# Moving 228 stores from SyncE's DMA queue to GpSimd's, and spreading eight squares over 14 steps

## The chip, the cores and the metric

The kernel runs on one core of one Trainium2 chip. The metric is the device time of one execution in microseconds (us). Three runs of the kernel before took 1536.45, 1539.39 and 1541.62 us, a median of 1539.39. The engines are named as the profile names them: PE (TensorE, matmuls; PEld are its weight loads), DVE (VectorE), ACT (ScalarE), POOL (GpSimd) and SP (SyncE, which here does nothing but issue DMAs).

## The reference

A decoder block on `x` (1 x 2048 x 1024, float32), one layer:

```python
xn = rms_norm(h, norm_w)                     # over 1024 features
proj = xn @ w_in                             # 1024 x 5632
u_a, z_a, q_b, f_b, i_b, og_b, z_b, g_a, g_b = split(proj)
y_a = s5_branch(u_a, z_a, ...)   # diagonal complex scan, GELU, GLU, times silu(z_a)
y_b = hgrn2_branch(q_b, f_b, i_b, og_b, z_b, ...)  # 4 gated recurrent heads, head norm, silu(z_b)
merged = sigmoid(g_a) * (y_a @ w_proj_a) + sigmoid(g_b) * (y_b @ w_proj_b)
h = h + merged @ w_out
return rms_norm(h, final_norm_w)
```

## The kernel before, in words

The 2048 tokens are worked in two halves `a` = 0 and 1 of 1024, each in two blocks `b` of 512. Matmuls run in float32r: every operand is split into a high and a low part (`split`, L118: ACT makes the high part at L119, DVE the low part at L120), and a product is three matmuls (high-high, high-low, low-high).

Projection. The columns of `w_in` are 22 slices of 256. The first two or three slices of the first half are done plainly (`plain`); all others by one level of Strassen's scheme (`strassen`, L425): seven products per slice, each one step of the dense loop with 12 matmuls (L458 to L460). Each product takes one weight operand of 128x1024, made by `w_ops` (L370) three products ahead, in a ring of five buffers (tag `wo`). In the first half `w_ops` makes the operands from raw weights (loads at L383) and also stores each to DRAM (`wc_d`, L391); the second half only loads them back (L375). PSUM banks are emptied on ACT by `snap` (L464), which copies a bank into an SBUF tile (`u`, `s`).

Tokens. The token statistics of a half are sums of squares: `norm_stats` (L178) loads rows of `xn` (L190) and squares them on ACT with a running sum (L191); `newton_rsqrt` (L149) on DVE makes the scale; `norm_diag` and `norm_bcast` spread it with one matmul. `xprep` (L239) then loads two tiles of transposed tokens (L243, L244; tag `y`, a ring of two buffers of 128x1024), scales them and forms the seven Strassen operands. For the first half they are split at once; for the second half they are stored to DRAM (`xo_d`, L257) and loaded back later by `x_load` (L287).

Other intermediate results also go through DRAM: the z gates (`silu_evac`, L863), the S5 output after GELU (`gelu`, L851), the state carried from the first half to the second (`hgrn_block`, L1042), the head outputs (`hgrn_fin`, L1084) and the b-branch part of the merge (`merge_b`, L1150). The sigmoid gates (`sg_d`, L875) and the S5 inputs and outputs are stored from ACT's queue. All other DMAs are issued from SP's queue.

Order. PE's instructions run in the order in which the program is written (`manual_schedule`, L1412); for the other engines and for the DMA queues a planner orders the instructions by priority and expected time, and each engine and queue then works strictly in order. The dense loop is a generator, and `timed` (L1372) runs background pieces (heads, statistics, token preparation) at numbered steps of it. For the first half's loop, the statistics of the second half's tokens come at steps 2 and 8 (L1482), their broadcasts at 13 and 18, and `xprep` of the second half from step 20 on. The kernel reserves 1024 bytes of SBUF per partition for descriptors of GpSimd's DMA queue, and issues no DMA there.

Of the kernel before, what the change touches and what calls it, by code (L numbers as in the profile page):

```python
# [11 lines left out]
F32 = mybir.dt.float32  # L12
# [3 lines left out]
AF = mybir.ActivationFunctionType  # L16
ALU = mybir.AluOpType
# [4 lines left out]
D = 1024  # L22
HALF = 1024
# [8 lines left out]
def hybrid_block(  # L32
# [24 lines left out]
    nc = tc.nc  # L57
    V = nc.vector
    S = nc.scalar
# [40 lines left out]
    def y4(name):  # L100
        return yp.tile([128, 1024], F32, name=name, tag="y")
# [13 lines left out]
    def r2(name, dt=F32R):  # L115
        return rp.tile([128, 512], dt, name=name, tag="r")
# [61 lines left out]
    def norm_stats(a, b):  # L178
        t0 = a * HALF + b * 512
        c0 = a * 8 + b * 4  # L180
        for i in range(4):
            rows = slice(t0 + i * 128, t0 + (i + 1) * 128)
            if a == 0:
                for h in range(2):
                    xr = r2(f"xr{a}{b}{i}{h}", F32)
                    nc.sync.dma_start(xr, xn[rows, h * 512 : h * 512 + 512])
                    S.activation(xr, xr, AF.Square, accum_out=ssh[:, h * 4 + i : h * 4 + i + 1])
            else:
                xr = y4(f"xr{a}{b}{i}")
                nc.sync.dma_start(xr, xn[rows, :])  # L190
                S.activation(xr, xr, AF.Square, accum_out=ssx[:, c0 + i : c0 + i + 1])  # L191
        if a == 0:
            V.tensor_tensor(ssx[:, c0 : c0 + 4], ssh[:, 0:4], ssh[:, 4:8], op=ALU.add)
        newton_rsqrt(ssx[:, c0 : c0 + 4], 4, 1.0 / D, rst[:, c0 : c0 + 4])

    def norm_diag(a, b):
        c0 = a * 8 + b * 4
# [41 lines left out]
    def xprep(a, k, rbs):  # L239
        t0 = a * HALF  # L240
        xa = y4(f"xa{a}{k}")
        xb = y4(f"xb{a}{k}")
        nc.sync.dma_start(xa, xt[k, :, t0 : t0 + HALF])  # L243
        nc.sync.dma_start(xb, xt[k + 4, :, t0 : t0 + HALF])  # L244
        (b11, b12), (b21, b22) = ((t[:, 0:512], t[:, 512:1024]) for t in (xa, xb))

        def scale(v, kk, b):
            V.scalar_tensor_tensor(v, v, nw_t[:, kk : kk + 1], rbs[b], op0=ALU.mult, op1=ALU.mult)

        def op(p, raw):  # L250
            n = f"X{a}{k}{p}"
            if a == 0:
                hi, lo = r2(n + "h"), r2(n + "l")
                split(raw, hi, lo)
                X[a][p][k] = (hi, lo)
            else:
                nc.sync.dma_start(xo_d[p][k // 2][:, (k % 2) * 512 : (k % 2) * 512 + 512], raw)  # L257

        scale(b11, k, 0)
        op(0, b11)  # L260
        yield
        scale(b21, k + 4, 0)
        op(1, b21)
        yield
        scale(b12, k, 1)
        scale(b22, k + 4, 1)
        yield
        t3 = sn(f"t3x{a}{k}")
        V.tensor_tensor(t3, b22, b12, op=ALU.subtract)
        V.tensor_tensor(b12, b12, b11, op=ALU.subtract)  # L270
        yield
        V.tensor_tensor(b11, b12, b22, op=ALU.subtract)
        op(2, b11)
        yield
        op(3, b12)
        yield
        op(4, t3)
        yield
        V.tensor_tensor(b21, b21, b11, op=ALU.add)
        op(5, b21)  # L280
        yield
        op(6, b22)
        yield
# [86 lines left out]
    def w_ops(a, sl):  # L370
        n = f"{a}_{sl}"
        if sl in wc_d:
            for p in range(7):
                t = wo4(f"w{n}_{p}")
                nc.sync.dma_start(t.bitcast(F32), wc_d[sl][p])  # L375
                yield t
            return
        if a == 0:
            wc_d[sl] = [dram.tile([128, 1024], F32, name=f"wc{sl}_{p}") for p in range(7)]

        def get(kh):
            raw = (y4 if a and sl != SL_VO else wr4)(f"rw{n}_{kh}").rearrange("p (k n) -> p k n", k=4)
            nc.sync.dma_start(raw, wi[sl, kh])  # L383
            return raw[:, :, 0:128], raw[:, :, 128:256]

        def op(p, raw):
            t = wo4(f"w{n}_{p}")
            v = t.rearrange("p (i k n) -> p i k n", i=2, k=4)
            split(raw, v[:, 0], v[:, 1])
            if a == 0:  # L390
                nc.sync.dma_start(wc_d[sl][p], t.bitcast(F32))  # L391
            return t

        a11, a21 = get(0)
        yield op(0, a11)
        a12, a22 = get(1)
        s1 = wpool.tile([128, 4, 128], F32, name=f"s1{n}", tag="wt", bufs=2)
        s2_ = wpool.tile([128, 4, 128], F32, name=f"s2{n}", tag="wt", bufs=2)
        t = op(1, a12)
        V.tensor_tensor(s1, a21, a22, op=ALU.add)  # L400
        yield t
        V.tensor_tensor(s2_, a11, s1, op=ALU.subtract)
        yield op(2, s2_)
        t = op(3, s1)
        V.tensor_tensor(a11, a11, a21, op=ALU.subtract)
        yield t
        t = op(4, a11)
        V.tensor_tensor(a12, a12, s2_, op=ALU.add)
        yield t
        yield op(5, a22)  # L410
        yield op(6, a12)
# [425 lines left out]
    def gelu(a, i):  # L837
        ya = wr4(f"ya{a}{i}")
        yy = y4(f"yy{a}{i}").rearrange("p (t c) -> p t c", t=8)
        nc.sync.dma_start(yy, y_d[a][i].rearrange("t p g c -> (p g) t c"))  # L840
        for i4 in range(4):
            c0 = i4 * 256
            dst = ya[:, c0 : c0 + 256] if i4 % 2 == 0 else ya[:, c0 + 255 : (c0 - 1 if c0 else None) : -1]
            S.activation(dst.rearrange("p (c t) -> p t c", t=8), yy[:, :, i4 * 32 : i4 * 32 + 32], AF.Copy)
        q = yy.rearrange("p t c -> p (t c)")
        S.activation(q, ya, AF.Square)
        V.tensor_scalar(q, q, 0.044715, 1.0, op0=ALU.mult, op1=ALU.add)
        V.tensor_tensor(q, q, ya, op=ALU.mult)
        S.activation(q, q, AF.Sigmoid, scale=GE)
        V.tensor_tensor(ya, ya, q, op=ALU.mult)  # L850
        nc.sync.dma_start(ft_d["ya", a, i], ya)  # L851

    def silu_evac(nm, a, i):
        def evac(ft, b, ps, sb):
            f = i * 2 + ft
            s = ps if sb is None else sb
            e = sn(f"e{nm}{a}{f}{b}")
            S.activation(e, s, AF.Sigmoid)
            if nm == "zb":
                V.scalar_tensor_tensor(e, s, hnw_t[:, f : f + 1], e, op0=ALU.mult, op1=ALU.mult)  # L860
            else:
                V.tensor_tensor(e, e, s, op=ALU.mult)
            nc.sync.dma_start(ft_d[nm, a, f][:, b * 512 : b * 512 + 512], e)  # L863

        return evac

# [66 lines left out]
    def hgrn_block(a, h, b):  # L933
# [105 lines left out]
            pv = ch(st, c)  # L1039
        st_prev[0] = pv  # L1040
        if a == 0 and b == NBLK - 1:
            nc.sync.dma_start(carry_d[h], pv)  # L1042
        yield
        ps = psm.tile([128, 512], F32, name=f"po{n}", tag="psm")
        for c in range(4):
# [20 lines left out]
    def hgrn_fin(a, h, direct=None):  # L1066
        o8 = (h % 2) * 8
        y = []
        for b in range(NBLK):
            y.append(sn(f"zy{a}{h}{b}"))  # L1070
            nc.sync.dma_start(y[b], ft_d["zb", a, h][:, b * 512 : b * 512 + 512])
        yield
        for b in range(NBLK):
            ys = h2(f"ys{a}{h}{b}", "x")
            for c in range(4):
                i = o8 + b * 4 + c
                S.activation(ch(ys, c), ch(OO[a, h, b], c), AF.Copy, scale=rso[:, i : i + 1])
            yield
            ps = psm.tile([128, 512], F32, name=f"py{a}{h}{b}", tag="psm")
            for c in range(4):  # L1080
                nc.tensor.transpose(ch(ps, c), ch(ys, c), ident)
            V.tensor_tensor(y[b], y[b], ps, op=ALU.mult)
            if direct is None:
                nc.sync.dma_start(ft_d["yb", a, h][:, b * 512 : b * 512 + 512], y[b])  # L1084
            else:
                direct(b, y[b])
            yield
# [26 lines left out]
    def merge_b(a):  # L1114
# [21 lines left out]
        for i, (jj, f, b) in enumerate(tiles):  # L1136
# [10 lines left out]
            mac12(ps, w, slice(f * 128, f * 128 + 128), [YB[a, k, b] for k in range(4)], (3,) if jj == 0 else range(4))  # L1147
            sg = sgs.pop(i)
            V.tensor_tensor(sg, sg, ps, op=ALU.mult)
            nc.sync.dma_start(ft_d["mb", a, j][:, b * 512 : b * 512 + 512], sg)  # L1150
            if i % 4 == 3:
                w = wn
            yield
# [244 lines left out]
    def steps(ev, g, at):  # L1398
        for t in at:
            ev.append((t, lambda: step(g)))  # L1400
        ev.append((at[-1], lambda: run(g)))
# [10 lines left out]
    with tc.manual_schedule(engines={mybir.EngineType.PE}):  # L1412
# [59 lines left out]
        def bcast(b):  # L1472
            rb1[b] = norm_bcast(1, b, dg1[b])
# [1 line left out]
        dg1 = {}  # L1475

        def stats(b):
            norm_stats(1, b)
            dg1[b] = norm_diag(1, b)

        ev = heads(0, 3, 35, 18)
        ev += [(2, lambda: stats(0)), (8, lambda: stats(1)), (13, lambda: bcast(0)), (18, lambda: bcast(1))]  # L1482
        xg = chain(*[xprep(1, k, rb1) for k in range(4)])
        steps(ev, xg, [20 + (s * 92) // 35 for s in range(36)])
        for i in range(6):
# [158 lines left out]
```

## Time and profile before

| | |
|---|---|
| median of three runs | 1539.39 us (1536.45 to 1541.62) |
| the profiled execution's own time | 1540.05 us |
| its span, first to last instruction | 1538.3 us |
| PE, PEld busy | 1467.0, 1207.3 us |
| DVE, ACT, POOL busy | 1100.8, 637.6, 3.6 us |
| mean granted TensorE clock | 0.984 |
| moved by DMA | 354.53 MB, 230 GB/s over the span |
| DMAs of SP and ACT (shares of 16 DMA engines) | 63.6%, 4.8% |

The profile is of one execution. Busy time is the union of an engine's instructions. A view of waits says for how long an engine stood idle before an instruction, and whose end released it. The granted clock is a share of TensorE's full speed: 1.00 is 2.4 GHz, 0.50 is 1.2 GHz, and a stretch between them held both. The DMA share is the mean busy share of the 16 DMA engines.

### The profile page before, as it was taken

What the parts mean: (1) busy time and instruction counts of PE and PEld (TensorE: products, weight loads), DVE (VectorE), ACT (ScalarE), POOL (GpSimd) and SP (SyncE); (2) the same over time, 40 slices, a digit from 0 to 9 for tenths busy, and PEclk for the clock granted to TensorE, in tenths of its full rate; (3) what the DMA queues carried; (4) which work ended last, traced back from release to release, by engine and by line L of the source; (5) the groups of instructions that cost most, each with busy time, mean ns of one, the idle gap of its engine ahead of it and who ended that gap; (6) DMA issues with size and microseconds to landing.
All of it is one profiled execution on the core that took longest, in us unless ns stands there. A gap on an engine that the chain in (4) does not pass through costs nothing.

```text
span 1538.3 us, 21386 instructions
## 1 busy us (share of the span) xinstructions
PE 1467.0 (95%) x7360; PEld 1207.3 (78%) x7360; DVE 1100.8 (72%) x2409; ACT 637.6 (41%) x1391; POOL 3.6 (0%) x24
## 2 busy tenths in 40 slices
PE   7997999999999999999989999999989899899997
PEld 5776788788888777878878887788878688688886
DVE  5798688678678659956665887776649877765445
ACT  7456454454454634323323455333353332532222
POOL 0000000000000000000000000000000000000000
PEclk9998999999999999999999999999999999999999
DMA  9539778977977883786668559677977854854602
GB/s 336 175 115 305 284 278 295 316 255 269 331 264 286 285 271 119 186 245 197 231 201 313 174 163 294 217 259 264 327 236 234 266 184 137 274 171 131 212 14 103
DMA packets 192060, 354.53 MB, mean 230 GB/s; under 512 B 65680, under 2 KB 74896, under 8 KB 191952
## 3 DMA queue, kind: packets, MB, share of 16 engines
q1 hardware_dynamic: 163792, 328.00, 63.6%
q10 hardware_dynamic: 28160, 25.17, 4.8%
q8 instruction: 58, 0.95, 0.3%
q14 instruction: 50, 0.41, 0.1%
HBM read 214.17 MB, written 138.94 MB: 230 GB/s over the span
## 4 chain that ended last, share of the span: by engine, by line
PE 68%; DVE 15%; DMA 10%; ACT 3%; issue 3%; SPq 0%; ACTq 0%; DVEq 0%
PE pd L458 14%; PE pd L460 13%; PE pd L459 13%; PE pf L1284 3%; PE pf L1285 3%; PE pf L1286 3%; PE pp L1112 2%; PE pp L1111 2%; PE pp L1110 2%; PE sc L979 2%; DMA y_d<-T 1%; DVE w L120 1%; DMA xb<-in_xt_dram 1%; DMA xq<-xo_d 1%; PE pd L355 1%
## 5 line engine op out<-in xcount | busy, mean ns | idle before, releaser
L119 ACT ACTIVATE w<-rw 128x512 fp32r<-128x512 f32 x110 | 68.7, 628 | 112.7 <-PE pd L460 67.9
L1284 PE MATMUL pf<-ho,mh 128*128 128x512 f32 x256 | 101.2, 395 | 5.2 <-ACT mh L119 5.2
L1286 PE MATMUL pf<-ho,ml 128*128 128x512 f32 x256 | 100.6, 393 | 0.5 <-DVE ml L120 0.5
L1285 PE MATMUL pf<-lo,mh 128*128 128x512 f32 x256 | 100.3, 392 | 0.0
L464 ACT ACTIVATE u<-pd 128x512 f32<-128x512 f32 x80 | 47.5, 594 | 106.0 <-PE pd L460 103.3
L120 DVE TENSOR_TENSOR w<-rw,w 128x512 fp32r<-128x512 f32 x110 | 75.3, 685 | 16.9 <-ACT w L119 16.6
L467 DVE TENSOR_TENSOR u<-u,pd 128x512 f32<-128x512 f32 x80 | 54.8, 685 | 33.5 <-PE pd L460 22.8
L355 PE MATMUL pd<-xh,hw 128*128 128x512 f32 x128 | 52.4, 409 | 9.0 <-ACT hw L119 6.7
L1284 PEld LDWEIGHTS pf<-ho,mh 128*128 128x128 f32 x256 | 48.6, 190 | 15.4 <-ACT mh L119 5.5
L1286 PEld LDWEIGHTS pf<-ho,ml 128*128 128x128 f32 x256 | 48.4, 189 | 11.6 <-DVE ml L120 1.6
L1285 PEld LDWEIGHTS pf<-lo,mh 128*128 128x128 f32 x256 | 48.6, 190 | 9.9
L119 ACT ACTIVATE mh<-sgl 128x512 fp32r<-128x512 f32 x32 | 20.0, 629 | 86.7 <-DVE sgl L1227 86.3
L356 PE MATMUL pd<-xl,hw 128*128 128x512 f32 x128 | 51.2, 400 | 0.0
L357 PE MATMUL pd<-xh,lw 128*128 128x512 f32 x128 | 50.9, 397 | 0.0
L980 DVE COPY_PREDICATED s_buf<-masks,sc 128x256 f32<-128x256 uint8 x64 | 32.5, 508 | 25.0 <-PE sc L979 25.0
L1110 PE MATMUL pp<-yh,hpa 128*128 128x512 f32 x128 | 50.2, 392 | 0.0
L1112 PE MATMUL pp<-yh,lpa 128*128 128x512 f32 x128 | 49.9, 390 | 0.2 <-DVE lpa L120 0.2
L1111 PE MATMUL pp<-yl,hpa 128*128 128x512 f32 x128 | 50.0, 390 | 0.0
L1226 DVE TENSOR_TENSOR sgl<-sgl,pp 128x512 f32<-128x512 f32 x48 | 32.7, 683 | 23.0 <-PE pp L1112 22.9
L1016 DVE TENSOR_TENSOR Q<-Q,t 128x256 f32<-128x256 f32 x96 | 40.5, 422 | 10.0 <-PE sc L991 9.9
L974 ACT ACTIVATE KX<-K 128x128 f32<-128x128 f32 x128 | 32.6, 304 | 35.6 <-DVE K L1017 26.3
L979 PEld LDWEIGHTS sc<-Q,KX 128*128 128x128 f32 x256 | 38.0, 189 | 8.9 <-issue 1.8
(915 smaller groups left out, 4431.6 us busy)
## 6 DMA issues: line engine op xcount, KB each, us to landing
wc<-w SPq DMA_DIRECT2D x126, 512.0 KB, 3.4
w<-wc SPq DMA_DIRECT2D x126, 512.0 KB, 4.6
rw<-in_wi_dram SPq DMA_DIRECT2D x44, 512.0 KB, 4.6
sgl<-sg_d SPq DMA_DIRECT2D x48, 256.0 KB, 3.2
sg_d<-u ACTq DMA_DIRECT2D x32, 256.0 KB, 3.5
ro<-in_wo_dram SPq DMA_DIRECT2D x16, 512.0 KB, 5.1
hh<-in_xn_dram SPq DMA_DIRECT2D x32, 256.0 KB, 5.1
out_dram<-hh SPq DMA_DIRECT2D x32, 256.0 KB, 2.4
```

The lines of the kernel that those rows point to most:

```text
L119: S.activation(hi, raw, AF.Copy)
L120: V.tensor_tensor(lo, raw, hi.bitcast(F32), op=ALU.subtract)
L458: mm(o, w[:, 0, k], xh, start=(first and k == 0), stop=False, skip_group_check=True)
L459: mm(o, w[:, 0, k], xl, start=False, stop=False, skip_group_check=True)
L460: mm(o, w[:, 1, k], xh, start=False, stop=(k == 3), skip_group_check=True)
L979: mm(ps[:, :, c, :], ch(kx, c), qp, start=True, stop=True)
L1110: mm(ps, hi[:, k, fs], yh, start=(k == 0), stop=False)
L1111: mm(ps, hi[:, k, fs], yl, start=False, stop=False)
L1112: mm(ps, lo[:, k, fs], yh, start=False, stop=(k == last))
L1284: mm(o, mh[:, ts_], hi, start=(kk == 0), stop=False)
L1285: mm(o, mh[:, ts_], lo, start=False, stop=False)
L1286: mm(o, ml[:, ts_], hi, start=False, stop=(kk == 7))
```

## The change

Seven kinds of stores are issued from GpSimd's queue in place of SP's: operands `wc_d` (126), token operands `xo_d` (28), z gates (32), GELU (8), carries (4), head outputs (14), merge parts (16). The squares of the second half's tokens leave `norm_stats` and become a generator of ten pieces, run at steps 1 to 14: piece `i` squares tile `i`-2 and then loads tile `i`, in the same ring `y`. The two calls of `newton_rsqrt` move to steps 9 and 15, the first broadcast to step 12. In the second half the raw weights of the slices from `SL_QF` on use the ring `wr` (three buffers) in place of `y`; only one such slice besides `SL_VO` is concerned.

```diff
-            if a == 0:
-                for h in range(2):
-                    ...
-            else:
-                xr = y4(f"xr{a}{b}{i}")
-                nc.sync.dma_start(xr, xn[rows, :])
-                S.activation(xr, xr, AF.Square, accum_out=ssx[:, c0 + i : c0 + i + 1])
...
+    def norm_stats1():
+        tiles = {}
+        for i in range(10):
+            if i >= 2:
+                xr = tiles.pop(i - 2)
+                S.activation(xr, xr, AF.Square, accum_out=ssx[:, 6 + i : 7 + i])
+            if i < 8:
+                tiles[i] = y4(f"xr1{i}")
+                nc.sync.dma_start(tiles[i], xn[HALF + i * 128 : HALF + i * 128 + 128, :])
+            yield
...
-                nc.sync.dma_start(xo_d[p][k // 2][:, (k % 2) * 512 : (k % 2) * 512 + 512], raw)
+                nc.gpsimd.dma_start(xo_d[p][k // 2][:, (k % 2) * 512 : (k % 2) * 512 + 512], raw)
...
-            raw = (y4 if a and sl != SL_VO else wr4)(f"rw{n}_{kh}").rearrange("p (k n) -> p k n", k=4)
+            raw = (y4 if a and sl < SL_QF else wr4)(f"rw{n}_{kh}").rearrange("p (k n) -> p k n", k=4)
...
-                nc.sync.dma_start(wc_d[sl][p], t.bitcast(F32))
+                nc.gpsimd.dma_start(wc_d[sl][p], t.bitcast(F32))
...
         def stats(b):
-            norm_stats(1, b)
+            c0 = 8 + b * 4
+            newton_rsqrt(ssx[:, c0 : c0 + 4], 4, 1.0 / D, rst[:, c0 : c0 + 4])
             dg1[b] = norm_diag(1, b)

         ev = heads(0, 3, 35, 18)
-        ev += [(2, lambda: stats(0)), (8, lambda: stats(1)), (13, lambda: bcast(0)), (18, lambda: bcast(1))]
+        steps(ev, norm_stats1(), [1, 2, 4, 5, 7, 8, 10, 11, 13, 14])
+        ev += [(9, lambda: stats(0)), (12, lambda: bcast(0)), (15, lambda: stats(1)), (18, lambda: bcast(1))]
```

The stores at L851, L863, L1042, L1084 and L1150 change from `nc.sync` to `nc.gpsimd` in the same way.

## Rows read from the trace of the kernel before

**Rows 1.** The page: the span, and each engine's busy time.
```profile
span 1538.3 us, 21386 instructions
...
PE 1467.0 (95%) x7360; PEld 1207.3 (78%) x7360; DVE 1100.8 (72%) x2409; ACT 637.6 (41%) x1391; POOL 3.6 (0%) x24
```
**Rows 2.** PE's waits, whole span: for whom; us in total, times, longest.
```profile
PE pd L458 <- ACT u L464: 13.4, 4, 6.6
...
PE py L1081 <- ACT ys L1077: 5.7, 3, 2.3
...
PE pd L458 <- DMA w<-wc: 4.5, 2, 2.6
PE sc L967 <- DVE kl L120: 4.5, 1, 4.5
PE pv L1029 <- DVE st L1038: 3.4, 2, 2.0
```
**Rows 3.** Timeline of PE, 112 to 137 us: start, us, [idle before].
```profile
131.32 0.80 PE L458 MATMUL pd<-X004h,w 128*128 128x512 f32 x1 [6.60 <-ACT u L464]
```
**Rows 4.** Timeline of ACT, 96 to 160 us.
```profile
118.97 1.06 ACT L191 ACTIVATE xr<-xr 128x1024 f32<-128x1024 f32 x1 [2.78 <-DMA xr<-in_xn_dram]
...
129.23 1.06 ACT L191 ACTIVATE xr<-xr 128x1024 f32<-128x1024 f32 x1 [2.61 <-DMA xr<-in_xn_dram]
...
130.69 0.57 ACT L464 ACTIVATE u<-pd 128x512 f32<-128x512 f32 x1
```
**Rows 5.** The squares' line L191; last row: ACT's idle time before them, times.
```profile
L191 ACT ACTIVATE xr<-xr x8: 1047/1058/1063, 119.0 to 141.3; 128x1024 f32<-128x1024 f32 x8
...
  DMA xr<-in_xn_dram: 10.3, 5
```
**Rows 6.** Windows: length, busy PE, PEld, DVE, ACT, POOL; clock, DMA share, GB/s.
```profile
122.10:124.70 2.60, 2.60 (x14) 1.94 (x12) 2.00 (x6) 2.37 (x7) 0.00 (x0) 1.00 0.97 329
124.70:131.30 6.60, 0.02 (x1) 0.00 (x0) 4.66 (x13) 3.96 (x10) 0.00 (x0) 0.80 0.94 330
131.30:135.60 4.30, 4.28 (x10) 3.39 (x11) 2.10 (x12) 1.24 (x3) 0.00 (x0) 0.52 0.93 333
135.60:160.00 24.40, 24.40 (x122) 20.61 (x121) 23.22 (x71) 15.09 (x35) 0.00 (x0) 1.00 0.92 317
...
804.40:807.80 3.40, 3.40 (x8) 2.73 (x9) 2.68 (x5) 0.00 (x0) 0.10 (x1) 0.51 0.47 150
```
**Rows 7.** Waits of SP's queue, whole span.
```profile
SPq L391 <- DVE w L120: 173.3, 87, 8.3
```
**Rows 8.** The operand stores' line L391, 104 to 200 us: issues, landings.
```profile
L391 SPq DMA_DIRECT2D wc<-w x26: 319/320/450, 109.5 to 197.7; - x26
...
DMA to landing us min/median/max: 2.6/3.5/7.2
```
**Rows 9.** DMA issues, whole span: count, KB each, median us to landing.
```profile
wc<-w SPq DMA_DIRECT2D x126, 512.0 KB, 3.4
...
xr<-in_xn_dram SPq DMA_DIRECT2D x8, 512.0 KB, 4.7
```
**Rows 10.** The chain that ended last, in order of time: start, us, what.
```profile
293.26 4.26 DMA xo_d<-xb
297.54 6.82 DMA xb<-in_xt_dram
...
782.22 4.32 DMA sg_d<-s
786.56 5.07 DMA w<-wc
```
**Rows 11.** Timeline of SP, 768 to 812 us.
```profile
780.06 0.32 SPq L863 DMA_DIRECT2D zb_d<-ezb  x1
...
784.03 0.59 SPq L768 DMA_DIRECT2D E<-eh_d  x1
```
**Rows 12.** POOL's instructions by line: busy us, mean ns, idle before.
```profile
L820 POOL MEMSET T<- 128x4 f32 x8 | 0.8, 105 | 425.5 <-DVE t L816 394.9 <-PE pd L460 30.6
```

More of the change, by code (lines that the diff above doesn't have):

```diff
@@ L182, in norm_stats @@
             rows = slice(t0 + i * 128, t0 + (i + 1) * 128)
-            if a == 0:
-                for h in range(2):
-                    xr = r2(f"xr{a}{b}{i}{h}", F32)
-                    nc.sync.dma_start(xr, xn[rows, h * 512 : h * 512 + 512])
-                    S.activation(xr, xr, AF.Square, accum_out=ssh[:, h * 4 + i : h * 4 + i + 1])
-            else:
-                xr = y4(f"xr{a}{b}{i}")
-                nc.sync.dma_start(xr, xn[rows, :])
-                S.activation(xr, xr, AF.Square, accum_out=ssx[:, c0 + i : c0 + i + 1])
-        if a == 0:
-            V.tensor_tensor(ssx[:, c0 : c0 + 4], ssh[:, 0:4], ssh[:, 4:8], op=ALU.add)
-        newton_rsqrt(ssx[:, c0 : c0 + 4], 4, 1.0 / D, rst[:, c0 : c0 + 4])
+            for h in range(2):
+                xr = r2(f"xr{a}{b}{i}{h}", F32)
+                nc.sync.dma_start(xr, xn[rows, h * 512 : h * 512 + 512])
+                S.activation(xr, xr, AF.Square, accum_out=ssh[:, h * 4 + i : h * 4 + i + 1])
+        V.tensor_tensor(ssx[:, c0 : c0 + 4], ssh[:, 0:4], ssh[:, 4:8], op=ALU.add)
+        newton_rsqrt(ssx[:, c0 : c0 + 4], 4, 1.0 / D, rst[:, c0 : c0 + 4])
+    def norm_stats1():
[8 more added lines that the diff above has]
+            yield
     def norm_diag(a, b):
@@ L850, in gelu @@
         V.tensor_tensor(ya, ya, q, op=ALU.mult)
-        nc.sync.dma_start(ft_d["ya", a, i], ya)
+        nc.gpsimd.dma_start(ft_d["ya", a, i], ya)
     def silu_evac(nm, a, i):
@@ L862, in evac @@
                 V.tensor_tensor(e, e, s, op=ALU.mult)
-            nc.sync.dma_start(ft_d[nm, a, f][:, b * 512 : b * 512 + 512], e)
+            nc.gpsimd.dma_start(ft_d[nm, a, f][:, b * 512 : b * 512 + 512], e)
         return evac
@@ L1041, in hgrn_block @@
         if a == 0 and b == NBLK - 1:
-            nc.sync.dma_start(carry_d[h], pv)
+            nc.gpsimd.dma_start(carry_d[h], pv)
         yield
@@ L1083, in hgrn_fin @@
             if direct is None:
-                nc.sync.dma_start(ft_d["yb", a, h][:, b * 512 : b * 512 + 512], y[b])
+                nc.gpsimd.dma_start(ft_d["yb", a, h][:, b * 512 : b * 512 + 512], y[b])
             else:
@@ L1149, in merge_b @@
             V.tensor_tensor(sg, sg, ps, op=ALU.mult)
-            nc.sync.dma_start(ft_d["mb", a, j][:, b * 512 : b * 512 + 512], sg)
+            nc.gpsimd.dma_start(ft_d["mb", a, j][:, b * 512 : b * 512 + 512], sg)
             if i % 4 == 3:
```

## The prediction

> **What bounds the kernel now.** I read the page first: TensorE is busy for 1467.0 of the span's 1538.3 us, GpSimd for 3.6 [rows 1]. So no change that leaves the matmuls alone can win more than some 70 us, and what can be won stands in the list of TensorE's own waits, which I read second: it sums to about 63 us. Its largest line, 13.4 us, is an eviction on ScalarE (`u`, L464) that frees a PSUM bank too late, 6.6 us of it in a single place [rows 2]. Third came the timelines around that place. TensorE stops at 124.7 us and goes on at 131.32 [rows 3]. ScalarE meanwhile sits in front of a square of the token statistics (L191) whose load has not landed, runs it at 129.23, and evicts only at 130.69, since it works in order [rows 4]. The eight squares cost ScalarE 10.3 us of such waiting in five places [rows 5]. Fourth, the windows give the granted clock: after the stop the matmuls ran for 4.3 us at 0.52, which is the 1.2 GHz level for nearly all of it, and before and after at 1.00 [rows 6]. Last, the SP queue, which issues nearly all transfers in order: 173.3 us of its time pass in front of the operand stores, waiting for the split (L120) that makes the data [rows 7].
>
> **Part 1, the squares.** Before, `norm_stats(1, b)` puts four loads of 128x1024 and four squares directly behind each other, over a ring of two buffers (`y`), at steps 2 and 8. After, ten small pieces run at steps 1 to 14, and a square follows its load by two pieces, that is by two or three steps of the dense loop. A step is about 3.5 us here: 26 operand stores, one for each step, issue between 109.5 and 197.7 us, 88.2 us for 25 intervals [rows 8]. The load takes 4.7 us to land [rows 9], so it is there when ScalarE comes to the square after 7 us or more. ScalarE's work stays the same (8 squares of 1.06 us and their read-outs); only the waiting goes. `newton_rsqrt` now starts at steps 9 and 15, its broadcasts at 12 and 18, three steps or 10 us later; the scaled tokens that need them start at step 20, as before, so nothing there becomes late.
>
> What it is worth at most: the wait of 6.6 us, and what the low clock took, 4.3 us x (1 - 0.52) = 2.1 us; together 8.7 us. What is late next is VectorE. From 122.1 to 160.0 us it is busy 2.00 + 4.66 + 2.10 + 23.22 = 32.0 of 37.9 us [rows 6]. If TensorE comes 8.7 us earlier, only 29.2 us are there for it, 2.8 too few, and the products of this stage wait for its splits: 8.7 - 2.8 = 5.9 us remain. The transfers give the lower end. Their share over the same four windows, weighted, is 0.93, 35.2 us of full use; in 29.2 us that is 6.0 too much, and 8.7 - 6.0 = 2.7 us remain, if none of them may slide. Many may: the loads of tokens are for later steps. I take VectorE's 5.9 us, since in this stage it has no work that can be dropped, and keep 2.7 and 8.7 as ends. The other stop here, 4.5 us for `kl` (L967, at 118.66) [rows 2], is VectorE's own backlog and stays.
>
> **Part 2, the stores.** 228 stores leave SP for GpSimd: 126 of 512 KB for the weight operands [rows 9], 28 for the token operands, 32 z gates, 8 GELU, 4 carries, 14 head outputs and 16 merge parts. In the stage of the first half's products, which writes the operands, SP's waits cost TensorE nearly nothing: of all its waits only the two below are for a transfer [rows 2]. So most of the 173.3 us is cover that nobody needed, and I count it at 0.
>
> The place where SP matters is near 790 us: two waits for `w<-wc`, 2.6 and 1.9 us, 4.5 in all [rows 2]. The chain shows why: the load of operands is issued at 786.56, as soon as the gate store `sg_d<-s` of ScalarE's queue, begun at 782.22, has landed [rows 10]. The two share no tile, so I read it as a completion counter that the transfers of both queues use in turn: an issue waits until an earlier transfer on its counter has landed. The z store at 780.06 is one of the turns in between; without it the wait falls to the next issue, and the weight load could go behind the one at 784.03, which ends at 784.62 [rows 11]: 1.9 us earlier. The second wait has stores of `cs_d` in front of it, which stay on SP. Ends: 0, and 4.5 us with the clock's share behind it, 3.4 us x (1 - 0.51) = 1.7 [rows 6], 6.2 in all. I take 1.9.
>
> What the stores cost on GpSimd no row shows: its queue issues no transfer here. The nearest rows are SP's issue, 0.32 us [rows 11], and as the far end the slowest landing of such a store, 7.2 us [rows 8]; below nothing is possible too, since a store no longer waits for what stands ahead of it on SP. I take about 1 us of extra landing, near the SP row. GpSimd's own work, 3.6 us in 24 instructions, is no competitor, but its memsets (L820, in the SSM chain) now stand behind stores that wait for their data; they are 105 ns each [rows 12] and their batch has steps to spare, so I count 0. The Trainium skill, "DMA: Bandwidth & Descriptors", section "Specifications", gives about 1 us to the first byte from GpSimd's queue against 0.6 from SP's; by that a store lands 0.4 us later, and the cost below would be 0.4 instead of 1.0. No run here shows it.
>
> Where would later landing be felt? An operand tile comes back after five steps, 17.6 us; two splits and the landing take 1.4 + 3.5 us, at worst 1.4 + 7.2 [rows 8], so some 9 us cover it: 0. The token buffers are tighter. At 293.26 us a store of `xo_d` runs 4.26 us, the load of the next pair waits for it and takes 6.82 [rows 10], VectorE stands in front of its first use, and TensorE then waits 2.0 us for `st`, the longest of that line's 3.4 [rows 2]. There are three such hand-overs, and one reached TensorE: at 1 us of extra landing I count 1.0 us, with ends of -0.5 and 3.8 (7.2 less the usual 3.4).
>
> The changed buffer for two weight loads of the second half (`wr` for `y`) touches four loads near 580 us; the list of TensorE's waits names no load there [rows 2], so 0.
>
> **The sum.** 5.9 + 1.9 - 1.0 = 6.8 us off the profiled execution's 1540.05: 1533.3. That execution is 0.7 us above the median of 1539.39, so against the medians 1532.6; I say 1532.5. From the ends: gains of 8.7 + 6.2 + 0.5 to 2.7 + 0 - 3.8, that is 1524 to 1540.
>
> **The rivals.**
> B, more than that goes. If the free SP queue brings all its loads forward, 8.7 + 6.2 us go, and with them the 2.3 us at 540 us in which `py` waits for `ys` [rows 2] behind late token loads: 17.2 us, 1522. For it: 173.3 us of waiting on SP. Against it: in the stages with these waits TensorE was hardly ever short of a load.
>
> C, no change: the wait moves and the stores did not matter. TensorE loses the wait for the eviction and gets one for a split, at VectorE or at the transfers: 2.7 us for part 1, 0 for part 2, less 1.0: 1538. For it: VectorE at 23.22 of 24.4 us and transfers at 0.92 directly behind [rows 6]. The Trainium skill, "DMA: Bandwidth & Descriptors", "Issuing engines are not separate DMA queues", says that issuing from several engines only saves the sequencer's time to start a transfer. By that rule part 2 is 0; the waits of SP in rows 7 are no such time, but the store rows stood on no path to the end, so the trace agrees in most places.
>
> D, slower: GpSimd's queue becomes the bound. While the operands are made, from 54 to 514 us, but in earnest from 109.5 on, 126 + 28 + 16 + 6 = 176 of the stores fall into some 405 us: one every 2.3 us. If GpSimd needs less for one, nothing is felt; above that its queue falls behind, the five operand tiles are not given back, and all steps run at its pace. At 2.4 us that is 176 x 0.1 = 17.6 us, so 1550; at 7.2 us it would be hundreds. For it: these stores wait in order for VectorE's data, and no row tells their price. Against it: SP does the same at 0.32 us each, and the cover of 9 us.
>
> **Chances.** The forecast 0.41, with its own range 1526 to 1537; B 0.14; C 0.24; D 0.21. 0.3% (4.6 us) is about what a measurement of this kernel can tell from no change. Faster by more than that is nearly all of the forecast and B, 0.54; within it is C and the upper edge of the forecast, 0.25; slower is D, 0.21. For 8 in 10 the range runs from a little below B, 1518, to the mild form of D, 1548; the rest is a worse D and a better B.
>
> **What would show it.** Right for part 1: ScalarE's idle time in front of the squares falls from 10.3 us to under 2, the wait for `u` near 125 us is gone, and the clock stays at 1.00 behind it; wrong, if a wait for a split by VectorE of similar length stands there. Right for part 2: no SP wait for `w` at the stores, GpSimd issues under 1 us apart where stores stand in line, landings of 4 to 5 us, and `w<-wc` waits of under 3 us. The prediction as a whole is wrong if TensorE has new waits for splits or operand tiles between 160 and 480 us, where it now has the 2.0 us at `st` alone.

## The result, and the profile after

The changed kernel takes 1559.54 us against 1538.97 us for the kernel before, measured beside it (medians): the ratio is 1.013, with a 95% interval from 1.0115 to 1.0145. It is 20 us slower; 1532.5 was forecast.

The page of the changed kernel, the span and the busy times, to stand beside [rows 1]:
```profile
span 1557.7 us, 21532 instructions
...
PE 1473.5 (95%) x7360; PEld 1210.8 (78%) x7360; DVE 1098.0 (70%) x2409; ACT 637.3 (41%) x1391; POOL 126.6 (8%) x252
```
TensorE is busy 6.5 us more for the same 7360 matmuls (its mean granted clock is 0.979, before 0.984), and its waits sum to 76 us instead of 63: together the 19.4 us by which the span grew. GpSimd has 126.6 us of work; 228 of its 252 instructions are the stores.

TensorE's waits in the changed kernel (us in total, times, longest), to stand beside [rows 2]:
```profile
PE po L1051 <- DVE st L1043: 11.1, 4, 5.2
PE pd L463 <- ACT u L469: 9.2, 3, 6.5
...
PE sc L996 <- DVE Q L1021: 5.5, 1, 5.5
...
PE pd L463 <- DMA w<-wc: 4.8, 2, 3.5
PE sc L972 <- DVE kl L120: 4.5, 1, 4.5
PE py L1086 <- ACT ys L1082: 3.4, 2, 2.0
```
The wait for `u` fell by 4.2 us. New at the top is `po`, which waits for VectorE's `st`. So the next view is what VectorE itself waits for. First the changed kernel:
```profile
DVE s L405 <- DMA rw<-in_wi_dram: 33.2, 17, 5.1
...
DVE T L699 <- DMA T<-in_cre_dram: 6.7, 1, 6.7
```
and the same two waits in the kernel before:
```profile
DVE s L400 <- DMA rw<-in_wi_dram: 4.9, 5, 1.8
...
DVE T L694 <- DMA T<-in_cre_dram: 0.6, 1, 0.6
```
This is the clearest difference between the two traces: `s` is the sum with which VectorE, beside the split of that half (L120), begins its work on the second half of a weight slice. There are 22 of them, and VectorE now stands 28 us longer in front of them. VectorE has idle time enough (70% busy), but it works in order, so what is queued behind `s` stands too.

One such place, VectorE's timeline of the changed kernel (start us, us, [idle before]):
```profile
305.35 0.34 DVE L1043 SCALAR_TENSOR_TENSOR st<-st,t,pv 128x128 f32<-128x128 f32 x1
310.17 0.69 DVE L405 TENSOR_TENSOR s<-rw,rw 128x512 f32<-128x512 f32 x1 [4.48 <-DMA rw<-in_wi_dram]
310.78 0.34 DVE L1043 SCALAR_TENSOR_TENSOR st<-st,t,pv 128x128 f32<-128x128 f32 x1
...
312.50 0.34 DVE L1043 SCALAR_TENSOR_TENSOR st<-st,t,pv 128x128 f32<-128x128 f32 x1
```
TensorE at that place:
```profile
312.89 1.23 PE L1051 MATMUL po<-V,s_buf 128*128 128x128 f32 x4 [5.23 <-DVE st L1043]
```
The same place in the kernel before:
```profile
307.57 1.50 DVE L1038 SCALAR_TENSOR_TENSOR st<-st,t,pv 128x128 f32<-128x128 f32 x4
308.98 0.69 DVE L400 TENSOR_TENSOR s<-rw,rw 128x512 f32<-128x512 f32 x1
```
Before, the four `st` stood ahead of `s`; the load had landed when VectorE came to `s`. After, `s` stands ahead of three of them. The load wasn't there, VectorE stood 4.48 us, and TensorE 5.23 us. About 2 us of the 4.48 are the load's own: at this place it landed 7.8 us after its issue, before 5.8.

Is the load late, or is `s` early? The landings of all 44 loads of raw weights for the Strassen slices, changed kernel first, then the kernel before (us from issue, min/median/max):
```profile
DMA to landing us min/median/max: 3.5/4.6/8.7
```
```profile
DMA to landing us min/median/max: 3.5/4.6/7.1
```
On the whole they land as fast as before: those of the 22 second halves take 112.3 us together, before 107.5, and 115.6 in the kernel of the first experiment below, which has all stores on SP. Nor are they issued much sooner, though SP has fewer stores to hand out: counted in matmuls that TensorE has begun by then, the median load is issued one matmul earlier than before, single ones up to 63 earlier or 40 later. SP's waits in the changed kernel:
```profile
SPq L388 <- DVE w L120: 165.4, 19, 17.0
```
The 173.3 us that SP stood in front of the stores [rows 7] now stand in front of these loads: their buffer comes free with the same split (`w`, L120). So in the main the loads come when they came, and `s` is early.

Set against each other matmul by matmul (start in the one trace less start of the same matmul in the other), the changed kernel is 6.2 us ahead of the kernel before at 140 us, and then loses in steps: 1.6 ahead at 200, 5.1 behind at 320, 10.4 at 460, 15.0 at 700, 19.1 at the end.

### The profile page after: what moved, and what is told of

It reads as the page before. It is cut to its first block, busy times and chain, and to the rows that moved or that the text cites. A ratio compares the mean times of both kernels' runs of the same rounds, so it can differ in the third digit from the quotient of the medians.

```text
span 1557.7 us, 21532 instructions
## 1 busy us (share of the span) xinstructions
PE 1473.5 (95%) x7360; PEld 1210.8 (78%) x7360; DVE 1098.0 (70%) x2409; ACT 637.3 (41%) x1391; POOL 126.6 (8%) x252
## 4 chain that ended last, share of the span: by engine, by line
PE 56%; DVE 17%; DMA 13%; issue 9%; ACT 4%; SPq 1%; ACTq 0%; POOL 0%; DVEq 0%; POOLq 0%
PE pd L463 11%; PE pd L464 10%; PE pd L465 10%; PE pf L1289 3%; PE pf L1290 3%; PE pf L1291 3%; DMA rw<-in_wi_dram 2%; PE pp L1115 2%; PE pp L1117 2%; PE pp L1116 2%; DMA xr<-in_xn_dram 2%; DVE w L120 1%; PE sc L984 1%; DMA w<-wc 1%; DMA gy<-ya_d 1%
## 5 line engine op out<-in xcount | busy, mean ns | idle before, releaser
L396 POOL DMA_DIRECT2D wc<-w x126 | 67.4, 535 | 361.3 <-DVE w L120 224.1
L120 DVE TENSOR_TENSOR w<-rw,w 128x512 fp32r<-128x512 f32 x110 | 75.1, 685 | 17.3 <-ACT w L119 17.2
```

What stands on the lines that cost most here:

```text
L120: V.tensor_tensor(lo, raw, hi.bitcast(F32), op=ALU.subtract)
L396: nc.gpsimd.dma_start(wc_d[sl][p], t.bitcast(F32))
```

## The experiments

What the kernels differ in besides the queue is the order of instructions, which the planner writes for every engine but TensorE. Theory Order says that this order costs the time; theory Landing, that the stores do it on GpSimd's queue; theory Squares, that the other half of the change does. Ratios are to the kernel before, with 95% intervals. In the texts below "252 stores" should be 228: 24 of the 252 are GpSimd's own instructions.

**One half of the change at a time.** The squares alone, on the changed kernel:
```diff
-nc.gpsimd.dma_start(...)      # at all seven places
+nc.sync.dma_start(...)
```


> The changed kernel with all seven stores back on SyncE's queue: only the squares over 14 steps (and the raw-weight ring that goes with them) are left of the change. Theory Order (the loss comes from the order that the planner writes for VectorE once the stores are off SyncE: the first op on a raw weight half is put ahead of ops that TensorE waits for, and stands there until its load lands, 33.2 us in 17 waits against 4.9 in 5) and theory Landing (the stores land 1.6 us later from GpSimd's queue, 5.0 against 3.4 us, and free buffers late): both expect the gain of the squares without the loss, 1539 - 6 = 1533 (1530 to 1536), and VectorE's wait for raw weights back near 5 us. Theory Squares (the spread squares upset the order themselves, stores or not): 1550 or more, with the 33 us wait still there.

Measured: 1537.16 us, ratio 0.9964 (0.9946 to 0.9983). By 1539 us that is 5.5 us off. Theory Squares falls. VectorE's wait for raw weights, and ScalarE's for the squares' loads (last row, to set beside the last of [rows 5]):
```profile
DVE s L405 <- DMA rw<-in_wi_dram: 8.6, 6, 2.0
```
```profile
  DMA xr<-in_xn_dram: 3.4, 2
```

The stores alone, on the kernel before:
```diff
-nc.sync.dma_start(...)        # the same seven places
+nc.gpsimd.dma_start(...)
```


> The kernel before with only its seven stores moved to GpSimd's queue; squares as before. Order and Landing: the whole loss without the gain, 1539 + 20 + 6 = 1565 (1555 to 1570), VectorE waiting some 30 us for raw weights under Order, about 5 us under Landing (there the waits are for buffers that stores hold). Squares: 1539.

Measured: 1573.9 us, ratio 1.0199 (1.0172 to 1.0226). So the stores cost 31 us by themselves, where 26 were expected. VectorE waits 23.5 us for raw weights, and the same new line stands among TensorE's waits:
```profile
PE po L1046 <- DVE st L1038: 9.9, 4, 3.7
```

The stores in two parts, on the changed kernel:
```diff
 # e3: only these stay on GpSimd's queue; e4: all but these
 nc.gpsimd.dma_start(wc_d[sl][p], t.bitcast(F32))
```


> The changed kernel with only the weight operands' stores (126 of 252) on GpSimd's queue, the six other kinds on SyncE's. Order: these stores stood among the raw-weight loads on SyncE, so taking them out is what moves the loads' consumers forward: most of the loss, 1548 to 1558, VectorE's wait for raw weights over 20 us. Landing: the operand ring has 9 us of slack, so these stores cost nothing: 1533 to 1537.

> The other half: all stores but the weight operands' on GpSimd's queue. Order: little of the loss, 1533 to 1542, VectorE's wait for raw weights under 15 us. Landing: nearly all of it, 1550 to 1560, in waits for x tiles, z gates and y buffers that a late store holds.

Measured: 1554.6 us, ratio 1.0077 (1.0052 to 1.0102) with the operand stores, 1546.44 us, ratio 1.0018 (1.0000 to 1.0036) with the others. Over the squares alone that is 17 and 8 us, together 25.7, about what all of them cost in the changed kernel, (1.013 - 0.9964) x 1539 = 25.5 us. VectorE's waits for raw weights, first with the operand stores, then with the others on GpSimd:
```profile
DVE s L405 <- DMA rw<-in_wi_dram: 31.6, 18, 4.4
```
```profile
DVE s L405 <- DMA rw<-in_wi_dram: 12.3, 12, 2.4
```

**The order alone.** Each engine's instructions can be chained in a given order, by edges that fix the order of issue and nothing else:
```diff
+for a, b in zip(line, line[1:]):     # an engine's instructions, in the order wanted
+    tc.add_manual_dep(b, a.name, info, reason="held")
```


> The changed kernel, all 252 stores on GpSimd's queue, but VectorE, ScalarE and SyncE's loads are held to the order that they have in the kernel with the squares alone (the run with all stores back on SyncE, ratio 0.9964). Theory Order (the loss is the order that the planner writes once it counts SyncE as free): the loss is gone, ratio 0.994 to 1.000, 1530 to 1539, VectorE's wait for raw weights back under 12 us. Theory Landing (the loss is what the stores do on GpSimd's queue: they land later, hold buffers longer, share the DMA engines with the loads): the loss stays, ratio 1.010 or more, 1555 or more.

Measured: 1539.06 us, ratio 0.9980 (0.9960 to 1.0000). With every store on GpSimd, 23 of the 25.5 us are gone. The stores' landing is still the long one, and VectorE's wait is the short one:
```profile
wc<-w POOLq DMA_DIRECT2D x126, 512.0 KB, 5.1
```
```profile
DVE s L405 <- DMA rw<-in_wi_dram: 8.8, 5, 2.6
```
Theory Landing falls for all but the last 2.5 us, and there the intervals of this run and of the squares alone overlap.

> The mirror of it: all stores on SyncE's queue, but VectorE, ScalarE and SyncE's loads are held to the order of the changed kernel; the stores stand where the planner puts them. Order: the loss is there without one store on GpSimd, ratio 1.008 to 1.018, 1552 to 1567, VectorE waiting some 30 us for raw weights. Landing: ratio 0.996, 1533.

Measured: 1588.93 us, ratio 1.0281 (1.0255 to 1.0306): the loss is there without one store on GpSimd, as theory Order has it, but nearly twice as large as expected. VectorE's wait:
```profile
DVE s L405 <- DMA rw<-in_wi_dram: 47.3, 17, 8.7
```
Here the order was made for a queue without stores, and SP has them all.

> As the first of these, but only VectorE is held to the order of the kernel with the squares alone; ScalarE and SyncE stand as the planner now puts them. Order, with VectorE as the engine whose places matter: ratio 0.995 to 1.002. Order, with SyncE's loads as the ones that matter (the loads issue in another order): 1.006 or more. Landing: 1.010 or more.

Measured: 1555.88 us, ratio 1.0075 (1.0052 to 1.0098): neither reading as it stood. Matmul by matmul against the squares alone, this kernel is 2.9 us behind at 680 us, where the changed kernel is 19.1 behind: up to there VectorE's order is nearly all of it. Then it loses 11.4 us at one place near 830 us, where VectorE, held to the one order, meets a load that SP issues in the other, and some 10 us more between 1100 and 1340 us. VectorE's wait at the one place:
```profile
DVE s L405 <- DMA rw<-in_wi_dram: 14.1, 1, 14.1
```

**Sixteen instructions.** In the programs as built, 16 of the 22 `s` (L405) stand further ahead in the changed kernel than with the squares alone. The first run moves these 16 of VectorE's instructions (the raw-weight loads may slide with them: 65 of SP's 944 DMAs stand in another place), the second puts them back:
```diff
 # h5: squares alone, all stores on SP, VectorE and ScalarE held to their own order
-  ... st, st, st, s<-rw,rw (L405) ...
+  ... s<-rw,rw (L405), st, st, st ...     # 16 times, by 3 to 25 places
```


> The kernel with the squares alone, all stores on SyncE's queue, VectorE and ScalarE in its own order, but for 16 of VectorE's instructions: the first op on a raw weight half (22 of them) is put ahead of the 3 to 25 instructions that it stands ahead of in the changed kernel; raw-weight loads may slide a place on SyncE, all other loads keep theirs. Theory First op (these 16 places make the loss): ratio 1.003 to 1.012, 1545 to 1558, VectorE's wait for raw weights over 25 us. Theory Whole order (the loss is spread over many places on VectorE, ScalarE and SyncE): ratio 0.996 to 1.000, about 1535 to 1540.

Measured: 1575.02 us, ratio 1.0212 (1.0182 to 1.0243). 16 instructions of VectorE's 2400, moved a few places ahead, cost 2.5%, 38 us. That is more than twice the middle of the range (17 us over the squares alone). The waits of VectorE and SP point to the reason:
```profile
DVE s L405 <- DMA rw<-in_wi_dram: 53.1, 19, 8.3
```
```profile
SPq L396 <- DVE w L120: 188.9, 83, 11.6
```
SP's wait was 172.1 us with the squares alone. With the stores on SP a weight load can stand behind a store that waits for VectorE, while VectorE stands for the load: the one issued at 411.32 us goes right behind a store issued at 410.95, lands at 417.99, and VectorE stands 3.2 us for it. That this makes up all of the excess isn't shown.

```diff
 # h4: the changed kernel, planned anew
+for a, b in BEHIND:                    # 16 pairs: s (L405), the instruction to stay behind
+    tc.add_manual_dep(dve[a], dve[b].name, info, reason="held")
```


> The mirror: the changed kernel with its stores on GpSimd's queue, planned anew with 16 added rules that keep those 16 instructions behind what they stand behind in the kernel with the squares alone. Theory First op: most of the loss is gone, ratio 0.998 to 1.005, 1537 to 1548, VectorE's wait for raw weights under 12 us. Theory Whole order: ratio 1.009 or more, 1554 or more.

Measured: 1547.63 us, ratio 1.0033 (1.0015 to 1.0052). The 16 rules take back (1.013 - 1.0033) x 1539 = 15 of the 25.5 us. The two waits, VectorE's and TensorE's:
```profile
DVE s L405 <- DMA rw<-in_wi_dram: 7.5, 5, 2.8
```
```profile
PE po L1051 <- DVE st L1043: 3.6, 2, 1.9
```
How much TensorE gets done between 160 and 700 us shows it in one row for each kernel (length; busy us of PE and number, then PEld, DVE, ACT, POOL; clock, DMA share, GB/s): the changed kernel, the one with the 16 rules, the squares alone, and the squares alone with the 16 moved ahead.
```profile
160.00:700.00 540.00, 517.24 (x2639) 424.05 (x2637) 400.85 (x941) 239.38 (x559) 97.99 (x187) 0.98 0.74 256
```
```profile
160.00:700.00 540.00, 526.39 (x2728) 433.34 (x2727) 407.38 (x952) 245.40 (x568) 98.16 (x187) 0.99 0.76 261
```
```profile
160.00:700.00 540.00, 526.81 (x2728) 433.21 (x2727) 404.89 (x938) 242.30 (x563) 0.95 (x6) 0.99 0.77 262
```
```profile
160.00:700.00 540.00, 512.32 (x2575) 419.35 (x2573) 393.82 (x928) 236.40 (x546) 0.94 (x6) 0.98 0.73 251
```
In 540 us TensorE does 2639 matmuls in the changed kernel, 2728 once the 16 are back, and 2728 with the squares alone. In this stretch the 16 account for the whole loss. What the 16 rules don't give back is lost on either side of it: set against the squares alone, that kernel is 5.0 us behind at 160 us already (it waits 2.9 us for `u` near 130 us), 5.1 at 1000 and 14.9 at 1360. (The profiled execution of the squares alone took 1532.52 us, 4.6 less than its median, so these distances are some us too long.)

**What the queue itself costs.** The two parts of the stores again, now in the order of the squares alone.

> Only the weight operands' stores on GpSimd's queue, with VectorE, ScalarE and SyncE's loads in the order of the kernel with the squares alone. With the planner's own order this set cost 17 us over the squares alone (ratio 1.0077 against 0.9964). Theory Order: 0.995 to 0.999. Theory Landing: 1.005 or more.

> The six other kinds of store on GpSimd's queue, the weight operands' on SyncE's, with the same order held. In the planner's own order this set cost 8 us over the squares alone (1.0018 against 0.9964). Theory Order: 0.995 to 0.999. If what is left with all stores on GpSimd in the held order (0.9980 against 0.9964, some 2.5 us) comes from their later landing, it is these that hold x tiles and y buffers: 0.998 here and 0.996 with the weight operands alone; otherwise the other way round.

Measured: 1534.54 us, ratio 0.9951 (0.9934 to 0.9968) with the operand stores, 1539.26 us, ratio 0.9979 (0.9962 to 0.9995) with the others. Both kernels are chained, so the chaining itself costs nothing that could be told. The operand stores cost nothing on GpSimd's queue once the order is kept, where the planner's order had cost 17 us. The others may cost some 2 us; the intervals overlap with that of the squares alone, so this stays open. The operand stores in the held order make the fastest kernel of all; it can't be told from the squares alone, and both beat the kernel before and the changed one.

## Why the prediction was wrong

**The step that failed** is the one on SP's waits in part 2: "So most of the 173.3 us is cover that nobody needed, and I count it at 0." For the queue by itself the 0 was right: in the held order all stores on GpSimd's queue measure 0.9980 and all on SP 0.9964, and SP in the changed kernel waits 165.4 us for the buffers of the loads instead. But the sum took the order of the instructions on the other engines as given. It isn't: the planner writes it anew for every change, and with the stores off SP it puts VectorE's first op on a weight half ahead of work that TensorE waits for. This term was missing. It measures 23 us, which is what holding the order takes back; rules on 16 instructions alone take back 15. The sign that the prediction had named for being wrong came with it: between 160 and 480 us TensorE waits 9.0 us in three places with `po` for `st`, where before it waited 2.0. Why the planner does so, no trace shows; that it takes the loads to come earlier when their queue is free is argued, not shown.

**Part 1, the squares:** 5.9 us forecast, 5.5 measured by themselves (2.6 to 8.3 from the interval). The stop of [rows 3] is gone there, the `kl` stop stays at 4.5 us, and what is next is small: the other two waits from 110 to 165 us are 0.6 us each, for a split and for an eviction, and before they were 0.6 and 0.4. That the two numbers meet is in part luck: matmul by matmul the squares alone gain 7 us on the kernel before between 120 and 160 us, so the 2.8 us that VectorE was to take back there aren't seen; they give some 3.5 back between 460 and 700 us and gain as much again between 1100 and 1340. ScalarE's idle time before the squares fell to 3.4 us, not under 2. In the changed kernel as a whole it did not fall at all: 12.9 us in 6 waits, with the squares' loads landing after 6.0 instead of 4.7 us; even so, TensorE gained 5.4 us on the kernel before between 120 and 140 us, and gave 3 of them back by 160.

**Part 2, near 790 us:** 1.9 us forecast, and in sum nothing came: the waits for `w<-wc` are 4.8 us in two, where they were 4.5 [rows 2]. But the step held for the first of them, and what failed is that the second was taken to stay. TensorE's two waits before, the same two in the changed kernel, and SP's two issues there that the forecast named:
```profile
791.76 0.47 PE L458 MATMUL pd<-X104h,w 128*128 128x512 f32 x1 [2.60 <-DMA w<-wc]
...
804.40 0.80 PE L458 MATMUL pd<-X106h,w 128*128 128x512 f32 x1 [1.94 <-DMA w<-wc]
```
```profile
805.49 0.47 PE L463 MATMUL pd<-X104h,w 128*128 128x512 f32 x1 [1.34 <-DMA w<-wc]
...
819.70 0.80 PE L463 MATMUL pd<-X106h,w 128*128 128x512 f32 x1 [3.50 <-DMA w<-wc]
```
```profile
799.02 0.70 SPq L773 DMA_DIRECT2D E<-eh_d  x1
799.77 0.50 SPq L380 DMA_DIRECT2D w<-wc  x1
```
The load now goes directly behind `eh_d`, as forecast. In all 13 profiles of these kernels the first wait is 2.5 to 3.3 us with the z stores on SP and 1.3 to 1.8 us with them on GpSimd; the second is 1.3 to 1.9 us with them on SP (and in four of these six a third follows, of 1.4 to 1.8) and 3.2 to 5.8 with them on GpSimd. So the z stores did hold the first load, and without them the wait moved to the second. The reading of a counter used in turn holds as well: before, the load of 786.56 us waits for the very semaphore that the gate store of 782.22 raises when it lands, while GpSimd's stores raise others. In the held order SP stands there 3.2 us for a gate store (`sg_d<-eg`) before it issues operand loads, and the two waits sum to 7.4 us.

**Part 2, the price of the queue:** about 1 us more to land was taken; the operand stores land 1.6 us later, 5.0 against 3.4 [rows 9], an issue takes 0.53 instead of 0.32 us. The cover of 9 us for the operand ring was right: in the held order those stores cost 0. The hand-overs of token buffers were counted at 1.0 us with an end of 3.8. In the held order they cost nothing that shows: that kernel is 1.6 us ahead of the squares alone at 460 us and 0.4 ahead at 700. It falls 2.5 us back between 700 and 800 us, where the waits for `w<-wc` are; as a time, the 2 to 2.5 us aren't resolved.

**The rivals.** The result lies on D's side, by another mechanism. D needs more than 2.3 us for a store on GpSimd's queue; the rows of the changed kernel give the price (operand stores from 104 to 200 us, ns min/median/max, then what ended GpSimd's idle time before them):
```profile
L396 POOL DMA_DIRECT2D wc<-w x26: 531/532/542, 109.0 to 195.9; - x26
...
  DVE w L120: 46.3, 14
```
At 0.53 us each GpSimd stands idle most of the time. B's gain isn't there even in the held order (0.9980). C had the stores right for the queue by itself, at nothing, and the squares too low. Its remark that the store rows stood on no path to the end holds for the operand stores alone: [rows 10] has a token store, `xo_d<-xb`, on that chain, and two stores of merge parts (`mb_d<-sgb`, 5.34 and 2.27 us near 565 us) stand on it too.

The Trainium skill, "DMA: Bandwidth & Descriptors", section "Issuing engines are not separate DMA queues", says that a second issuing engine saves no more than the sequencer's time to start a transfer. The held order agrees: 0.9980 with the 228 stores on GpSimd, 0.9964 with all on SP; nothing was won. The Trainium skill, "DMA: Bandwidth & Descriptors", section "Specifications", gives a first byte after about 1 us from GpSimd's queue against 0.6 us from SP's. No run here shows the first byte; the whole way to landing is 1.6 us longer for the operand stores, so the estimate of 0.4 us that the prediction made of it was too low.

**What stays open:** the rest of the loss. Against the profile of the squares alone, 4 to 5 us of it lie before 160 us, and some 8 to 9 between 1080 and 1360 us. The later part is there in the changed kernel, with the 16 rules, and with VectorE's order held. With ScalarE and SP's loads held as well it is gone in the run with all stores on GpSimd's queue, but in the run with the six other kinds alone, in the same held order, 6.8 us of it are there. Each is one profiled execution, and those of the squares alone and of the held order with all stores ran 4.6 and 3.6 us below their medians. So it isn't shown whether the order of ScalarE and SP, the six other kinds of store, or chance between executions makes it.

## What to carry to other kernels

Where a planner writes the order, moving a transfer to another queue is an edit of every engine's order: lay the two orders side by side, and look for ops on freshly loaded data that have moved ahead of work that the bounding engine waits for. An in-order engine that is 70% busy can still cost the bounding engine 20 us, if what it stands in front of is late. To price a queue by itself, hold the order and change the queue alone; and keep the part of a change that stands on a wait seen in the profile (here the squares, 0.9964), not the part that only clears a queue: the wait that this took from one load near 790 us came back at the next.

## What was not expected of the hardware

- 126 stores of 512 KB from GpSimd's queue land 1.6 us later than from SP's (5.0 against 3.4 us) and cost no time in the held order (0.9951).
- With 228 stores on GpSimd's queue the loads of raw weights land after the same median, 4.6 us, as with none. The gate stores of ScalarE's queue (`sg_d<-u`) land later, after 4.5 us; before it was 3.5, with the squares alone 3.9.
- A few instructions' places weigh more than a queue: 16 of VectorE's ops, 3 to 25 places ahead, cost 38 us, while 228 stores moved in the held order cost some 2.5 us, which is within the noise.
